# A trunk of two blocks on one core: the second block's adaptive sums on the vector engine behind the norm, one root for two norms, its attention regrouped, weights in 2 MB transfers

## The chip, the cores and the metric

One core of a Trainium2 chip runs the whole program. The metric is the device time of one execution in microseconds (us). Three executions of the kernel before gave a median of 1782.59 us (1780.39 to 1788.25). All arithmetic is float32.

## The reference

A row of 256 tokens of width 1024 passes through two blocks. Every sublayer is `x + gate * f(norm(x) * (1 + scale) + shift)`, where shift, scale and gate are an adaptive product of the conditioning vector with a 1024 x 3072 matrix.

```python
def adaln(cond, w, b):
    mod = cond @ w + b
    shift, scale, gate = jnp.split(mod, 3, axis=-1)
...
def attend(q, k, v):                 # attention a of the second block, 4 heads, two score maps each
    s = jnp.einsum('bqhcd,bkhcd->bhcqk', q, k) * (A_QK ** -0.5)
    p = jax.nn.softmax(s, axis=-1)
    a = p[:, :, 0] - lam * p[:, :, 1]
    return jnp.einsum('bhqk,bkhd->bqhd', a, v)
def post(o):
    o = rmsnorm(o, subln_g) * (1.0 - lam_init)
```

The first block has a Fourier and convolution mixer, a mixture of 16 experts with fixed capacity, a windowed attention and another such mixture. The second block's mixer has four groups of 256 channels: the attention `a` above (keys from 256 context and 256 own tokens), an attention `b` with a windowed bias, a pooling and a long convolution ("hyena"). Then come 16 experts of inner width 512, each token going to two of them, and a last norm.

## The kernel before

The stages run one after the other: mixer 0, experts 0, mixer 1, experts 1, mixer 2, experts of the second block (`moe2`), the last norm. In this profile they are at 0 to 155, 184 to 641, 654 to 772, 799 to 1265, 1266 to 1468 and 1490 to 1765 us.

All weights, 631 MB, come in one fixed order through a ring. `Stream.pump` (L309) issues the next transfer on SP's queue as long as fewer than `RING` slots are taken. A slot is 1 MB, 128 partitions of 2048 floats, and there are 14. `done` frees a slot once its last reader is issued; the transfer that takes its place waits for that reader. The host lays the weights out so that one slot is one contiguous block (`by_rows`, L257).

The adaptive products are cut into steps by `ada_steps` (L480). Where `ON_V` names a part, VectorE adds up the rows of the matrix into the first slot (`add_rows`, L485: the first row of 1024 columns by L492, each further one by L490), and one short set of matmuls with ones sums over the partitions (L497). Elsewhere TensorE does it, for shift and scale at L512 and for the gate at L555. For the second block, keys (2, 0) and (2, 1), TensorE does all of it. `fill` takes the next of these steps wherever the program calls it, so these calls set where the products stand among the other work; `weave` steps through several generators in turn. The order on each engine is then fixed by a scheduler when the program is built.

Mixer 2 (`mixer2`, L1351) takes the roots of two norms, one after the other (`rstd`, `inv_root`), scales, turns and modulates the rows (L648, L659, L671), projects them (L1395 with rope, L1337 for features, L1325 for tokens), and then weaves attention `a` with further projections and hyena with attention `b` and pooling. In both attentions a step is one head of 128 queries: scores (L1436 or L1500), softmax on VectorE and ScalarE, four transposes of the weights (L1419), and four matmuls with the values into 128 queries by 64 channels (L1423). The results of both are then turned at L1373. The output product is L697, the sums over the norm's squares L614.

In `moe2` the router (L681 to L963), a chain of small VectorE operations (L1672 to L1826) and the gathers (L1743) come ahead of the first expert. An expert has L1772 (two products into halves of the columns), L1787 and L1797, and L1802 multiplies by the gate row `hkb`.

```python
RING = 14
ON_V = {(0, 0): "", (0, 1): "s", (1, 0): "g", (1, 1): "sg", (2, 0): "", (2, 1): ""}
```

## Time and profile before

| | |
|---|---|
| median of three executions | 1782.59 us (1780.39 to 1788.25) |
| the profiled execution | 1785.29 us, its span 1783.1 us |
| TensorE (PE) busy | 1421.8 us, 80% of the span |
| VectorE (DVE) / ScalarE (ACT) busy | 455.2 us, 26% / 242.9 us, 14% |
| weights on SP's queue | 630.67 MB, engines taken 86.6% of the span |
| mean granted TensorE clock | 0.857 of full speed |

The profile counts two records for one float32 matmul or weight load of the program (a transpose has one), so "x32" of L697's shape is 16 matmuls. A busy share is an average over stages with different limits, so every stage is read by itself.

### The profile page before, as it was taken

What the parts mean: (1) busy time and instruction counts of PE and PEld (TensorE: products, weight loads), DVE (VectorE), ACT (ScalarE), POOL (GpSimd) and SP (SyncE); (2) the same over time, 40 slices, a digit from 0 to 9 for tenths busy, and PEclk for the clock granted to TensorE, in tenths of its full rate; (3) what the DMA queues carried; (4) which work ended last, traced back from release to release, by engine and by line L of the source; (5) the groups of instructions that cost most, each with busy time, mean ns of one, the idle gap of its engine ahead of it and who ended that gap; (6) DMA issues with size and microseconds to landing.
All of it is one profiled execution on the core that took longest, in us unless ns stands there. A gap on an engine that the chain in (4) does not pass through costs nothing. (4 is left out here: it accounts for less than half of the span.)

```text
span 1783.1 us, 24944 instructions
## 1 busy us (share of the span) xinstructions
PE 1421.8 (80%) x10776; PEld 720.3 (40%) x10776; DVE 455.2 (26%) x1042; ACT 242.9 (14%) x556; POOL 10.7 (1%) x19
## 2 busy tenths in 40 slices
PE   6997877867666679987676776678799998999996
PEld 2444423323222234543232232235477745655453
DVE  2523212401010038541110100100333424333223
ACT  3021100100000012420200000000222312101012
POOL 0000000000000000000000000000000000000000
PEclk9997868878676689998787767868898998999998
DMA  9978899999999999289999999999931566999970
GB/s 375 421 310 325 346 420 421 420 421 421 420 422 421 420 410 408 101 354 420 421 420 421 421 420 421 421 421 420 409 107 51 206 242 239 421 421 415 392 297 25
DMA packets 89746, 635.93 MB, mean 357 GB/s; under 512 B 10944, under 2 KB 11072, under 8 KB 13344
## 3 DMA queue, kind: packets, MB, share of 16 engines
q1 hardware_dynamic: 87392, 630.67, 86.6%
q0 software_dynamic: 1952, 3.09, 0.5%
q8 instruction: 87, 1.43, 0.3%
q10 hardware_dynamic: 288, 0.52, 0.1%
q14 instruction: 27, 0.22, 0.0%
HBM read 633.25 MB, written 1.05 MB: 356 GB/s over the span
## 5 line engine op out<-in xcount | busy, mean ns | idle before, releaser
L1052 PE MATMUL b<-w,xg 128*32 128x256 f32 x4096 | 359.3, 493 | 172.6 <-DMA w<-in_moe_w_up_dram 99.8
L1052 PEld LDWEIGHTS b<-w,xg 128*32 128x32 f32 x4096 | 135.9, 132 | 392.7 <-DMA w<-in_moe_w_up_dram 150.2
L1052 PE MATMUL b<-w,hidT 128*32 128x256 f32 x2048 | 173.8, 476 | 71.5 <-DMA w<-in_moe_w_down_dram 55.3
L1072 DVE TENSOR_TENSOR hid<-b,sg 128x256 f32<-128x256 f32 x32 | 13.6, 425 | 499.0 <-PE b L1052 406.6
L1052 PEld LDWEIGHTS b<-w,hidT 128*32 128x32 f32 x2048 | 64.8, 130 | 166.6 <-DMA w<-in_moe_w_down_dram 95.3
L1772 PE MATMUL u<-w,xg 128*64 128x256 f32 x1088 | 128.0, 383 | 0.0
L1080 DVE SCALAR_TENSOR_TENSOR Y<-b,cc,gq 32x256 f32<-32x256 f32 x128 | 61.5, 481 | 224.2 <-PE b L1052 222.6
L1772 PEld LDWEIGHTS u<-w,xg 128*64 128x64 f32 x1088 | 78.2, 137 | 46.1 <-issue 10.3
L1797 PE MATMUL b<-w,hidT 128*64 128x512 f32 x272 | 65.8, 598 | 6.0 <-ACT hidT L1789 6.0
L1067 ACT ACTIVATE sg<-b 128x256 f32<-128x256 f32 x32 | 12.3, 383 | 424.7 <-PE b L1052 424.7
L697 PE MATMUL b<-w,n 128*128 128x512 f32 x128 | 56.0, 594 | 0.0
L1077 ACT COPY hidT<-b 128x256 f32<-128x256 f32 x32 | 11.9, 372 | 312.2 <-PE b L1075 312.2
L490 DVE SCALAR_TENSOR_TENSOR w<-w,cond 128x1024 f32<-128x1024 f32 x42 | 52.4, 1276 | 1.3 <-DMA w<-in_ada01s_dram 1.2
L1743 PE MATMUL b<-oh,n 128*128 128x128 f32 (+1 forms) x288 | 40.8, 301 | 3.5 <-DVE oh L1737 2.1
L1093 PE MATMUL b<-Y,gT 128*128 128x512 f32 x64 | 35.7, 702 | 9.5 <-DVE Y L1080 9.5
L1174 PE MATMUL b<-w,hT 128*128 128x512 f32 x96 | 43.1, 605 | 0.0
L1743 PEld LDWEIGHTS b<-oh,n 128*128 128x128 f32 x288 | 38.0, 212 | 11.3 <-issue 7.9
L822 PE MATMUL b<-w,hT 128*128 128x512 f32 x96 | 41.6, 593 | 1.1 <-DVE hT L671 1.1
L989 PE MATMUL b<-oh,n 128*128 128x128 f32 x256 | 39.9, 323 | 0.9 <-DVE oh L1032 0.9
L989 PEld LDWEIGHTS b<-oh,n 128*128 128x128 f32 x256 | 37.3, 233 | 7.2 <-issue 5.7
L1325 PE MATMUL b<-pe,w 128*128 128x256 f32 x160 | 38.6, 396 | 0.0
L1802 DVE TENSOR_TENSOR Y<-b,hkb 64x512 f32<-64x512 f32 x34 | 23.4, 688 | 53.6 <-PE b L1797 53.3
(439 smaller groups left out, 1383.9 us busy)
## 6 DMA issues: line engine op xcount, KB each, us to landing
w<-in_moe_w_gate_dram SPq DMA_DIRECT2D x128, 1024.0 KB, 19.8
w<-in_moe_w_up_dram SPq DMA_DIRECT2D x128, 1024.0 KB, 19.8
w<-in_moe_w_down_dram SPq DMA_DIRECT2D x128, 1024.0 KB, 19.8
w<-in_moe_w_dram SPq DMA_DIRECT2D x102, 1024.0 KB, 10.4
w<-in_wi_dram SPq DMA_DIRECT2D x10, 1024.0 KB, 19.8
w<-in_ada00s_dram SPq DMA_DIRECT2D x8, 1024.0 KB, 18.5
w<-in_ada01s_dram SPq DMA_DIRECT2D x8, 1024.0 KB, 20.6
w<-in_ada10s_dram SPq DMA_DIRECT2D x8, 1024.0 KB, 7.0
```

Source lines behind the costliest of these rows:

```text
L490: V.scalar_tensor_tensor(into[:, hs], w[:, hs], c, into[:, hs], op0=OP.mult, op1=OP.add)
L697: T.matmul(acc, mixT[:, kt, b * 128:(b + 1) * 128], w(kt)[:, h * 512:(h + 1) * 512], start=kt == first, stop=kt == last)
L822: T.matmul(p, hT[:, kt, b * 128:(b + 1) * 128], w(kt), start=kt == 0, stop=kt == 7)
L989: T.matmul(p[:, j * 128:(j + 1) * 128], n[:, b, dt * 128:(dt + 1) * 128], oh[:, b, g * 128:(g + 1) * 128], start=b == 0, stop=b == 1)
L1052: T.matmul(p[32 * q:32 * q + 32, :256], lhs(kt), w[:, k, q * 256:(q + 1) * 256], start=kt == 0, stop=kt == 7)
L1080: V.scalar_tensor_tensor(Y[32 * j:32 * j + 32, q * 256:(q + 1) * 256], pd[32 * q:32 * q + 32, :256], cc[32 * q:32 * q + 32, e:e + 1], gq[3 ...
L1093: T.matmul(p, gT[:, b * 128:(b + 1) * 128], Y[:, h * 512:(h + 1) * 512], start=True, stop=True)
L1174: T.matmul(p, hT[:, kt, b * 128:(b + 1) * 128], w(kt), start=kt == 0, stop=kt == 7)
L1325: T.matmul(p[:, j * 256:(j + 1) * 256], w(kt)[:, c0 + j * 128:c0 + (j + 1) * 128], h[:, kt], start=kt == 0, stop=kt == 7)
L1743: T.matmul(p[:, j * 128:j * 128 + m], n[:, b, dt * 128:(dt + 1) * 128], oh[:, b, :m], start=b == 0, stop=b == 1)
L1772: T.matmul(p[rows[h], :256], xg[:, kt, c], w[kt // 4][:, kt % 4, h * 256:(h + 1) * 256], start=kt == 0, stop=kt == 7)
L1797: T.matmul(pd[rows[h]], hidT[:, kt % 2, rows[kt // 2]], w[kt // 2][:, kt % 2, h * 512:(h + 1) * 512], start=kt == 0, stop=kt == 3)
```

## The change

1. A transfer carries two slots, 2 MB with 16 KB for each partition, and the ring has 7 such tiles. A tile is freed when both halves are. What came alone (`tpc`, `dft`, `l0c`, `wbias`, `pool`) takes a whole tile; the two filter packs become one.
2. The second block's adaptive sums except shift and scale of (2, 0) go to VectorE: 8 + 16 + 8 operations on 1024 columns, and 4 + 4 + 2 matmuls with ones. `queue_behind` makes them stand behind the last VectorE operation of mixer 2's modulation, and in `moe2` behind the first gather's last `ohg`.
3. Both norms' mean squares stand in one tile of four columns, with one root.
4. A step of attention `a` is two heads, four score banks. The values are the stationary operand: two heads' products go to the two column halves, 64 channels by 128 queries, so the results come out turned; the norm of `a` and the division of `b` are applied through `spread`, 8 matmuls of 64 x 128 that copy a factor per head and query over the channels.
5. The calls of `fill` move: none before mixer 2's projections, five steps beside attention `a`, the rest beside hyena and `b`; in `moe2` the gate's steps come after the first pair's gather.

```diff
-ON_V = {(0, 0): "", (0, 1): "s", (1, 0): "g", (1, 1): "sg", (2, 0): "", (2, 1): ""}
-RING = 14
+ON_V = {(0, 0): "", (0, 1): "s", (1, 0): "g", (1, 1): "sg", (2, 0): "g", (2, 1): "sg"}
+RING = 7
...
     def pump(self):
-        while self.issued < len(self.order) and self.issued - len(self.freed) < RING:
...
+        while self.issued < len(self.order):
+            if self.issued - sum(all(k in self.freed for k in keys) for keys, _, _ in self.order[:self.issued]) >= RING:
+                return
+            keys, shapes, ap = self.order[self.issued]
+            t = self.pool.tile([128, 2 * SLOT], F32, name="w")
+            self.nc.sync.dma_start(t[:, :ap.shape[1]], ap)
...
         def add_rows(kt, w, into):
+            with ExitStack() as behind:
+                if queue_behind:
+                    behind.enter_context(tc.issue_after(queue_behind[-1].ins))
+                add_rows_(kt, w, into)
...
-            r1 = rstd(ss)
...
-            r2 = inv_root(r2)
-            V.tensor_tensor(r2, r2, r1, op=OP.mult)
-            fill(4)
+            ms = small.tile([128, 4], F32, name="r2")
...
+            rs = inv_root(ms, 4)
+            r1, r2 = rs[:, 0:2], rs[:, 2:4]
             scale_rows(n, x, r2)
-            modulate(hT, turn(n), ada[2, 0])
+            queue_behind.append(modulate(hT, turn(n), ada[2, 0]))
             scale_rows(x, x, r1)
-            fill_until(lambda: ((2, 0), "g", 3) in st.freed)
...
-                    T.matmul(po[:, h * 64:(h + 1) * 64], eT[:, kb * 128:(kb + 1) * 128], vals[:, kb, h * 64:(h + 1) * 64],
-                             start=kb == 0, stop=kb == 3)
+                    for u in range(2):
+                        h = 2 * j + u
+                        T.matmul(po[64 * u:64 * u + 64, at:at + 128], vals[:, kb, h * 64:(h + 1) * 64],
+                                 ets[u][:, kb * 128:(kb + 1) * 128], start=kb == 0, stop=kb == 3)
...
+                    pp = [bank() for _ in range(4)]
+                    for i in range(4):
+                        T.matmul(pp[i], qT[32 * i:32 * i + 32, j, qb * 128:(qb + 1) * 128], kT[32 * i:32 * i + 32, j], start=True, stop=True)
...
             def after_a():
+                A.activation(sq, oa, AF.Square)
...
-                t4(mixT[:, 0:2], lambda b: oa[:, b])
...
+                  fills(5))
+            fill_until(lambda: (2, 0) in gqs and ((2, 0), "g", 0) in st.freed)
+            weave(hyena(), attention_b(), after_a(), chain(pooling(), filling(1, (2, 1))))
...
-            fill(1)
             nT = [wk.tile([128, 8, 128], F32, name="xg", bufs=2) for _ in range(2)]
...
-            fill(99)
...
             ts = {0: pair(0)}
+            queue_behind.append(ts[0]["last"])
+            fill(99)
```

The change moves instructions. In its program the lines stand 10 to 35 further down: L555's work is L506 and L499, L659 is L668, L1395 L1404, L1436 L1463, L1419 L1428, L1423 L1440, L697 L707.

TensorE at the start of mixer 2, before (from the experts' last combination to the first scores):

```order
L1093 MATMUL b<-Y,gT 128x512 x4
L555 MATMUL b<-w,cond_both 32x256 x24
L659 MATMUL b<-cst,n 128x128 x6
L555 MATMUL b<-w,cond_both 32x256 x8
L659 MATMUL b<-cst,n 128x128 x10
L1395 MATMUL b<-w,pe 128x256 x32
L1337 MATMUL b<-w,pe 128x256 x16
L1325 MATMUL b<-pe,w 128x256 x16
L1373 MATMUL b<-cst,pe 128x128 x8
L1436 MATMUL b<-kT,qT 128x512 x4
L1325 MATMUL b<-pe,w 128x256 x8
L1419 MATMUL b<-cst,pe 128x128 x4
```

And in the changed kernel:

```order
L1103 MATMUL b<-Y,gT 128x512 x4
L668 MATMUL b<-cst,n 128x128 x16
L1404 MATMUL b<-w,pe 128x256 x32
L1347 MATMUL b<-w,pe 128x256 x16
L1335 MATMUL b<-pe,w 128x256 x16
L1383 MATMUL b<-cst,pe 128x128 x8
L1463 MATMUL b<-kT,qT 128x512 x8
L1335 MATMUL b<-pe,w 128x256 x16
L1428 MATMUL b<-cst,pe 128x128 x8
```

The 32 matmuls of the gate of (2, 0) are gone from around the transposes, and two steps of scores, eight banks, now stand in front of the next projection.

TensorE beside attention `b` and hyena, before (L512 is the shift and scale of (2, 1)):

```order
L1500 MATMUL b<-bk,bq 128x256 x4
L512 MATMUL b<-w,cond 32x512 x4
L1613 MATMUL b<-pe,w 128x256 x2
L1419 MATMUL b<-cst,pe 128x128 x3
L1613 MATMUL b<-pe,w 128x256 x6
L1419 MATMUL b<-cst,pe 128x128 x5
L512 MATMUL b<-w,cond 32x512
L1423 MATMUL b<-bv,pe 128x64 x8
L512 MATMUL b<-w,cond 32x512 x3
L1590 MATMUL b<-kT,w 128x256 x8
```

In the changed kernel, from attention `b`'s first scores (L1504 sums the squares of `a` over half the partitions, L1449 is `spread`):

```order
L1528 MATMUL b<-bk,bq 128x256 x8
L1504 MATMUL b<-cst,pe 128x2 x4
L1576 MATMUL b<-w,hcT 64x256 x8
L1610 MATMUL b<-kT,w 128x256 x8
L1428 MATMUL b<-cst,pe 128x128 x8
L1440 MATMUL b<-pe,bv 64x128
L1449 MATMUL b<-cst,root 64x128 x3
L1440 MATMUL b<-pe,bv 64x128 x7
L1449 MATMUL b<-cst,root 64x128 x5
```

No adaptive matmul is left between hyena's products and the attention, and L1504, which waits for ScalarE's square, stands in line ahead of hyena's L1610.

VectorE at the first gather of `moe2` in the changed kernel (L501 and L499 are the adaptive sum's operations, L1775 the modulated gather, L1762 and L1779 the one-hot tiles of the next pairs, L1809 an expert's hidden product); before, none of the sums stood there:

```order
L501 TENSOR_SCALAR w<-w,cond 128x1024
L1775 TENSOR_SCALAR xg<-b,shsc_7141 128x128
L499 SCALAR_TENSOR_TENSOR w<-w,cond 128x1024
L1775 TENSOR_SCALAR xg<-b,shsc_7141 128x128 x2
L499 SCALAR_TENSOR_TENSOR w<-w,cond 128x1024
L1775 TENSOR_SCALAR xg<-b,shsc_7141 128x128
L499 SCALAR_TENSOR_TENSOR w<-w,cond 128x1024
L1762 TENSOR_SCALAR oh<-cst,rank 128x64
L499 SCALAR_TENSOR_TENSOR w<-w,cond 128x1024
```

The sums now stand between the four evacuations that the first expert's products read.

## Rows read from the trace of the kernel before

**Rows 1.** The page: GB/s in 40 slices of 44.6 us each.

```profile
GB/s 375 421 310 325 346 420 421 420 421 421 420 422 421 420 410 408 101 354 420 421 420 421 421 420 421 421 421 420 409 107 51 206 242 239 421 421 415 392 297 25
```

**Rows 2.** DMA view of 250 to 600 us: all transfers, then SP's queue (packets, MB, share).

```profile
DMA packets 20207, 147.31 MB, mean 421 GB/s; under 512 B 2244, under 2 KB 2244, under 8 KB 2244
q1 hardware_dynamic: 20187, 147.00, 101.0%
```

**Rows 3.** Windows: stretch, its length, busy time per engine, clock, DMA share, GB/s.

```profile
1263.00:1286.00 23.00, 15.48 (x106) 7.16 (x107) 12.73 (x33) 8.97 (x22) 0.00 (x0) 0.68 1.01 420
1286.00:1382.00 96.00, 92.27 (x426) 72.14 (x425) 29.36 (x70) 23.32 (x55) 0.00 (x0) 0.95 0.27 97
1382.00:1440.00 58.00, 57.16 (x340) 38.78 (x339) 23.98 (x54) 18.52 (x40) 1.59 (x3) 1.00 0.69 245
1345.00:1356.00 11.00, 8.83 (x26) 6.02 (x26) 3.80 (x9) 1.93 (x5) 0.00 (x0) 0.54 0.16 63
1468.00:1498.00 30.00, 21.85 (x146) 15.34 (x144) 17.71 (x93) 6.49 (x15) 0.00 (x0) 0.83 0.54 205
1498.00:1740.00 242.00, 233.57 (x1604) 130.86 (x1602) 66.92 (x152) 30.32 (x73) 0.00 (x0) 1.00 0.94 382
```

**Rows 4.** Timeline of PE at mixer 2's start: start, length, line, idle before it.

```profile
1263.35 1.94 PE L1052 MATMUL b<-w,hidT 128*32 128x256 f32 x16 [0.55 <-DMA w<-in_moe_w_down_dram]
...
1281.42 1.51 PE L659 MATMUL b<-cst,n 128*128 128x128 f32 x6 [4.57 <-DVE n L648]
1282.87 1.83 PE L555 MATMUL b<-w,cond_both 128*32 128x256 f32 x16
```

**Rows 5.** Timeline of DVE in the two chained roots.

```profile
1277.83 0.16 DVE L1379 TENSOR_TENSOR r<-ss 128x2 f32<-128x2 f32 x1 [0.51 <-ACT b L614]
...
1280.53 0.75 DVE L648 TENSOR_SCALAR n<-x,root 128x1024 f32<-128x1024 f32 x1
```

**Rows 6.** Timeline of PE in attention `a`.

```profile
1315.22 1.14 PE L1436 MATMUL b<-kT,qT 32*128 32x512 f32 x8 [0.78 <-ACT kT L1374]
...
1346.51 1.11 PE L1419 MATMUL b<-cst,pe 128*128 128x128 f32 x4 [1.44 <-DVE pe L1452]
1348.36 1.97 PE L1423 MATMUL b<-va,pe 128*128 128x64 f32 x8 [0.73 <-ACT pe L1421]
...
1352.26 5.62 PE L1325 MATMUL b<-pe,w 128*128 128x256 f32 x16
...
1361.39 3.72 PE L1325 MATMUL b<-pe,w 128*128 128x256 f32 x16
```

**Rows 7.** PE groups by shape, 1300 to 1440 us: busy time, mean ns, idle before.

```profile
L1436 PE MATMUL b<-kT,qT 32*128 32x512 f32 x32 | 13.3, 702 | 0.8 <-ACT kT L1374 0.8
L512 PE MATMUL b<-w,cond 128*32 128x512 f32 x64 | 12.5, 603 | 0.0
...
L1423 PE MATMUL b<-va,pe 128*128 128x64 f32 x64 | 9.7, 299 | 0.7 <-ACT pe L1421 0.7
L1423 PE MATMUL b<-bv,pe 128*128 128x64 f32 x64 | 8.3, 278 | 0.7 <-ACT pe L1421 0.7
```

**Rows 8.** Timeline of PE in `moe2`: 32 matmuls into halves of the columns.

```profile
1647.10 7.08 PE L1772 MATMUL u<-w,xg 128*64 128x256 f32 x64
```

**Rows 9.** The page's group of VectorE's adaptive sums.

```profile
L490 DVE SCALAR_TENSOR_TENSOR w<-w,cond 128x1024 f32<-128x1024 f32 x42 | 52.4, 1276 | 1.3 <-DMA w<-in_ada01s_dram 1.2
```

**Rows 10.** DMA view of 697 to 800 us: issues, KB each, median us to landing.

```profile
w<-in_ada20s_dram SPq DMA_DIRECT2D x8, 1024.0 KB, 7.9
```

**Rows 11.** Timeline of DVE: the first two maxima of attention `a`.

```profile
1316.38 1.29 DVE L1442 TENSOR_REDUCE nm<-b 128x1 f32<-128x512 f32 x2 [14.57 <-PE b L1436]
```

**Rows 12.** Timeline of DVE in `moe2`'s router chain.

```profile
1483.11 0.69 DVE L563 TENSOR_TENSOR hkb<-b,hkb 128x512 f32<-128x512 f32 x1 [2.02 <-PE b L555]
```

**Rows 13.** Groups by shape, 1500 to 1760 us: PE's waits in the experts.

```profile
L1797 PE MATMUL b<-w,hidT 128*64 128x512 f32 x256 | 62.1, 598 | 5.5 <-ACT hidT L1789 5.5
...
L1787 PE MATMUL b<-cst,hid 128*128 128x128 f32 x32 | 7.0, 299 | 2.9 <-DVE hid L1783 2.9
```

More of the change, by code (lines that the diff above doesn't have):

```diff
@@ L80, in main_consts @@
     p.add("tri", (i[:, None] < i[None]).astype(float))
+    p.add("half", (i[:, None] // 64 == np.arange(2)[None]).astype(float))
     p.add("invf", np.tile(inv.astype(np.float32)[None], (128, 1)))
@@ L309, in pump @@
     def pump(self):
[L310 to L318 removed]
+        while self.issued < len(self.order):
[4 more added lines that the diff above has]
+            self.nc.sync.dma_start(t[:, :ap.shape[1]], ap)
+            for i, (key, shape) in enumerate(zip(keys, shapes)):
+                v = t[:, i * SLOT:i * SLOT + int(np.prod(shape))]
+                self.tiles[key] = v.rearrange("p (a b) -> p a b", a=shape[0]) if len(shape) == 2 else v
             self.issued += 1
@@ new lines, in mixer2, with scores, softmax @@
+            steps = [(qb, j) for qb in range(2) for j in range(2)]
+            def attention_a():
+                es = {}
+                po = bank()
+                def scores(qb, j):
+                    pp = [bank() for _ in range(4)]
+                    for i in range(4):
+                        T.matmul(pp[i], qT[32 * i:32 * i + 32, j, qb * 128:(qb + 1) * 128], kT[32 * i:32 * i + 32, j], start=True, stop=True)
+                    return pp
+                def softmax(pp, qb, j):
+                    nm = small.tile([128, 4], F32, name="nm2")
+                    for i in range(4):
+                        V.tensor_reduce(nm[:, i:i + 1], pp[i], axis=AX.X, op=OP.max, negate=True)
@@ new lines, in softmax @@
+                    e = []
+                    for i in range(4):
+                        e.append(temp())
+                        A.activation(e[i], pp[i], AF.Exp, scale=32 ** -0.5, bias=nm[:, i:i + 1], accum_out=den[:, i:i + 1])
+                    d = den.rearrange("p (u c) -> p c u", c=2)
+                    V.tensor_copy(den0[:, qb, 2 * j:2 * j + 2], d[:, 0])
+                    cf = small.tile([128, 2], F32, name="cf")
+                    V.reciprocal(cf, d[:, 1])
+                    V.scalar_tensor_tensor(cf, cf, lam, d[:, 0], op0=OP.mult, op1=OP.mult)
@@ L1466, in attention_a @@
+                    for u in range(2):
+                        V.scalar_tensor_tensor(e[2 * u], e[2 * u + 1], cf[:, u:u + 1], e[2 * u], op0=OP.mult, op1=OP.add)
+                    es[qb, j] = e[0::2]
                 softmax(scores(*steps[0]), *steps[0])
-                for t in range(8):
-                    if t < 7:
+                for t in range(4):
+                    if t < 3:
                         pp = scores(*steps[t + 1])
                     yield
-                    values(*steps[t])
-                    if t < 7:
+                    attend(po, es.pop(steps[t]), va, *steps[t])
+                    if t < 3:
@@ L1530, in attention_b @@
                     yield
-                    values(*steps[t])
+                    attend(po, es.pop(steps[t]), bv, *steps[t])
                     if t < 3:
@@ L1536, in attention_b @@
                         st.done(("wb", 0))
-                t4(mixT[:, 2:4], lambda b: ob[:, b])
-                after_a()
+                f = temp()
+                A.copy(f, spread(rd))
+                V.tensor_tensor(mixT[:, 2:4].rearrange("p j s -> p (j s)"), po, f, op=OP.mult)
             def short(g, j0):
@@ L1865, in pair @@
                 t = tiles()
-                take([(rank[:, :, e], gates[:, :, e]) for e in (e0, e0 + 1)], t)
+                t["last"] = take([(rank[:, :, e], gates[:, :, e]) for e in (e0, e0 + 1)], t)
                 return t
```

214 lines of the change are left out of this document (93 added, 121 removed).

## The prediction

> **What bounds the kernel now.** I read the page's slices first. Two long plateaus at 420 to 422 GB/s are the experts of the first block [rows 1]; the DMA view of one of them shows SP's queue taking 101.0% of the engines [rows 2], so there the weights are the bound and nothing an engine saves is worth anything. From the page's slices those plateaus are about 205 to 640 and 825 to 1263 us, 873 us together. The windows say what the second block is [rows 3]. From 1286 to 1440 us TensorE is busy 92.27 of 96 and 57.16 of 58 us while DMA stands at 97 and 245 GB/s: the ring is full and TensorE is the bound. At 1263 to 1286 (norm and roots) and 1468 to 1498 us (router) nothing is busy throughout and chains of small operations set the time, at a granted clock of 0.68 and 0.83. From 1498 to 1740 us TensorE is busy 233.57 of 242 us at 382 GB/s: TensorE first, transfers close behind. So the change can gain in the second block by taking work off TensorE, and what decides is whether waits appear where that work stood.
>
> **The transfers.** Bytes and their order stay. No row moves 16 KB for a partition, so the new rate is bounded by its neighbours. Below stand the page's slices of 410 GB/s at the ends of the plateaus [rows 1]: 873 x (421/410 - 1), +23 us. Above, of 20,207 packets 2,244 are under 512 bytes and close the transfers [rows 2]; half of them go, and if each took as long as one of data, 5.6% of 873 us would, -49. By their bytes, 512 at most, it is 0.4%. I take that, -3.5, since the engines' time follows the bytes at a steady 421. The Trainium skill ("DMA: Bandwidth & Descriptors", the fit under "Anatomy of one DMA") gives each transfer a fixed 2.0 us beside bytes / 436 GB/s; by it two slots in one transfer would cost 6.8 instead of 8.8 us, a quarter less. The rows have 1 MB in 2.49 us already (1.05 MB at 421 GB/s), so that fixed part is hidden, and the sum goes without it.
>
> A tile counts as landed only when both halves are. At the end of a plateau TensorE then has two slots to work through after the last landing instead of one: the last eight matmuls took 1.94 us [rows 4], 1 to 2 us more in each of two stages. At the start of each, the first freed tile needs both halves read, about 1 us. Together +5. In mixer 0 the last tile of the first shift and scale likewise leaves four more matmuls behind its landing, +1.
>
> **Mixer 2's start.** One root replaces two chained ones: from the second sum to the scaled rows took 2.70 us [rows 5], of which one square root and about three VectorE steps go, -0.65. The gate's last eight matmuls stood among the transposes for 1.83 us [rows 4]; they go. But the others kept TensorE at work before the wait of 4.57 us [rows 4]; without them it idles from 1272 us on, and the transposes begin at the low clock. I take -1.0 in all, between -2.5 and +1.
>
> **Projections and attention `a`.** Scores: four matmuls of 32 rows side by side took 1.14 us [rows 6], 1.07 from start to start, while all 16 took 13.3 us [rows 7], since later ones stood singly. Four groups of four are 4.3 us: -9.0. The Trainium skill ("TensorE: Matmul & The Clock Gate", part 3) measured four such matmuls 3.07 times as fast as singly; from the 1.05 us of a lone one the 16 would be 5.5 us by that. The row of this kernel decides. Values: 64 columns are half of the array; 32 matmuls of 256 columns into alternating halves took 7.08 us [rows 8], 0.22 each, so eight of 128 columns are about 0.9 us. Four steps are 3.6 against 9.7 us [rows 7]: -6.1. The two waits of 1.44 and 0.73 us and the clock of 0.54 that follows them [rows 3, 6] belong to the old grouping; sixteen records of L1325 took 5.62 instead of 3.72 us there: -4.6 for the whole dip. Added are four matmuls with ones, +0.5.
>
> Here a new wait comes in. The order puts two steps of scores, all eight banks of the kernel's pool, before the next projection, which therefore waits for the first exponential. Maxima take 0.64 us each and the first starts 1.16 us after the scores [rows 6, 11]. Four of them, the scaling and one exponential (taken as long as a maximum) end some 4.8 us after the scores start, and TensorE has 2.1 us of scores: +2.7. A wait of 1.44 us was followed by a clock of 0.54 for about 10 us [rows 3, 6], so I add +4.0 for a dip of that kind. This part: -9.0 - 6.1 - 4.6 + 0.5 + 2.7 + 4.0 = -12.5.
>
> VectorE has the room: its 24 sums of 1.28 us [rows 9] are 31 us beside 53 busy of 154 [rows 3]. Before rope six sums delay VectorE by at most 7.7 us, while TensorE has 21 us of projections, so they cost nothing. If ada21s lands late, VectorE waits in front of a softmax: a transfer of half the size took 7.9 us when alone [rows 10]. In attention `a` the next softmax has about that in hand.
>
> **Attention `b`, hyena, pooling.** L512 is busy for 12.5 us [rows 7], some 11.7 without the overlap of neighbouring records; it goes. Values go from 8.3 [rows 7] to 3.6, eight turnings go (1.2, from six transposes in 1.51 us at the low clock, [rows 4]); `spread` adds two times 0.9, the ones matmuls and the half sums 1.4. TensorE's work: -14.4. But L512 was also what TensorE did while softmax and hyena's VectorE steps ran. Now L1504 stands in line behind ScalarE's square, and the square behind the two exponentials of `b`'s first step: scores of 1.1 us, two maxima and their biases, two exponentials and the square, at 0.4 to 0.7 us each, end some 5 us after the scores start, of which TensorE has 2 covered, +3.0. VectorE's sums of the third ada21s tile come before those maxima and wait for a transfer issued late, +1.6. Hyena's products wait for VectorE operations that now stand behind `b`'s reciprocals and biases, and the last step and the ones matmuls wait for their softmax and copy: five waits of 0.4 to 1.3 us, +4.0. A clock dip as above, +4.0. This part: -1.8; without the dip and half of the waits it would be -10.
>
> **Router and `moe2`.** VectorE's chain stood 2.02 us for the gate and 0.69 in adding it [rows 12]; that moves behind the gather, -2.7. The table for roots, loaded earlier before, is now loaded right after the sums of squares, +0.9, and without the gate's matmuls TensorE's transposes and router products run at the low clock longer, +1.3. Sum -0.5. In `moe2` the first expert's inputs stand between sums of 1.28 us on VectorE and two ones matmuls wait for all eight sums, +2.9. The order of the later pairs has `hid` and `hidT` waited for in the open from the second pair on, where TensorE had 8.4 us of such waits [rows 13]: about 5 more waits of 0.55, less what fewer changes between shapes give back, +1.1. Sum +4.0. At the start five tiles of expert weights are in the ring instead of 14 slots; with TensorE asking for 382 of 421 GB/s [rows 2, 3] this lead is enough.
>
> **The sum.** +1.0 + 5.0 - 3.5 - 1.0 - 12.5 - 1.8 - 0.5 + 4.0 = -9.3 us against the profiled execution of 1785.3, which makes 1776.0. That execution is 2.7 above the median of the runs shown; against the median of 1782.6 the forecast is **1773.3 us**. A measurement of this kernel can tell about 0.5%, 9 us, from no change.
>
> **The rivals.**
> - *The work comes off whole.* No clock dips follow the new waits (-8) and the waits are half as long (-4): 1761 us. For it: the wait of 0.78 us at 1314 [rows 6] left the clock alone. Against it: the dip after 1.44 us.
> - *Attention `b` and hyena become chains.* TensorE waits in many pieces and falls to the low clock again and again in what was 1382 to 1440 us: a clock of 0.54 as at 1345 [rows 3] on 16 us of its work costs 16/0.54 - 16, 13.6 instead of the 4.0 taken, which makes 1783, no change. For it: with L512 gone softmax and hyena's steps have no cover, and that stretch was 98% busy [rows 3]. Against it: most of the work still stands between the waits. The Trainium skill ("TensorE: Matmul & The Clock Gate", part 1) says that the array falls to half its clock when it idles; by that rule this is what taking filler out costs, and [rows 3] agree with their 0.54.
> - *The larger transfers are slower.* 16 KB a partition at 410 GB/s: +23 in place of -3.5, 1800 us, slower than before. It decides from about 414 GB/s downwards, 873 x (421/414 - 1) = 15 us in place of -3.5. For it only the slices at the ends of the plateaus [rows 1]; against it the steady 420 to 422 between.
> - *`moe2` starves.* The gate's two tiles hold 4.2 MB of the ring into the first expert; if transfers then end last, the stage ends 4.2 MB / 421 GB/s later, +10: 1783. Against it: 382 GB/s asked [rows 3].
>
> **Chances.** Forecast 0.45, work comes off whole 0.25, chains 0.14, `moe2` starves 0.06, slower transfers 0.10. The forecast's own range is 1765 to 1781, and rather more than half of it lies below 1773.7, which is faster by 0.5%: 0.25, with the whole gain's 0.25 and 0.02 of the others 0.52. Slower by 0.5% (above 1791.5) are most of the slower transfers and the far end of the chains, 0.12. The rest, 0.36, is the same. The range that leaves out 2 in 10 reaches from 1755 to 1790.
>
> **What would show it.** After the change the two plateaus should show the rate (0.4% more taken); at 1310 to 1320 us TensorE should wait for the first exponential before the projection and the clock row dip after it; the scores should stand in groups of 1.1 us and the values at 0.9; L1504 should wait for ScalarE; in the router no wait for `hkb`. The forecast is wrong if the plateaus change by more than 5 us each, if mixer 2 from 1266 to 1440 us is not 12 to 20 us shorter, or if `moe2` is longer by more than 8.

## The result, and the profile after

The changed kernel takes **1761.98 us** (median of 4 runs, 1761.46 to 1762.87) against 1781.71 for the kernel before (4 runs): ratio 0.9883, 95% interval 0.9858 to 0.9907, 21 us faster by the ratio. The forecast was 1773.3 with a range of 1755 to 1790. The profiled execution took 1761.91 us with a span of 1760.0, so the sum is compared span with span: -23.1 us measured, -9.3 forecast.

The page of the changed kernel, GB/s in 40 slices of 44 us, and all packets:

```profile
GB/s 375 407 276 396 326 427 427 428 427 427 427 427 428 427 415 336 145 305 426 426 426 427 427 428 427 427 427 427 418 78 144 267 229 188 427 427 427 423 306 26
DMA packets 46973, 636.03 MB, mean 361 GB/s; under 512 B 6192, under 2 KB 6320, under 8 KB 8464
```

The plateaus stand at 427 where they stood at 421 [rows 1]. The DMA view of 250 to 600 us of the changed kernel, as [rows 2]:

```profile
DMA packets 10272, 149.57 MB, mean 427 GB/s; under 512 B 1142, under 2 KB 1142, under 8 KB 1142
q1 hardware_dynamic: 10252, 149.26, 100.3%
```

Half the packets for 1.5% more bytes. The windows of the second block, with the columns of [rows 3]: mixer 2's start, projections and attention `a`, attention `b` with hyena, the output projection and router, the experts.

```profile
1259.00:1276.00 17.00, 7.35 (x25) 4.84 (x26) 10.96 (x26) 9.23 (x22) 0.00 (x0) 0.70 0.96 406
1276.00:1359.00 83.00, 78.06 (x409) 63.16 (x408) 43.73 (x76) 21.83 (x51) 0.00 (x0) 0.98 0.27 95
1359.00:1413.50 54.50, 49.32 (x342) 38.32 (x341) 32.18 (x60) 22.30 (x45) 1.59 (x3) 0.97 0.73 289
1413.50:1471.00 57.50, 43.53 (x175) 27.33 (x174) 21.51 (x91) 9.97 (x21) 0.00 (x0) 0.82 0.36 139
1471.00:1710.00 239.00, 226.71 (x1580) 129.34 (x1580) 76.07 (x166) 28.44 (x71) 0.00 (x0) 1.00 0.97 405
```

In the second and third stretch TensorE does about 22 us less work than in 92.27 + 57.16 us before, but it now idles 5 us in each. The timeline of PE at the waits that the forecast named (start, length, line, in brackets the idle time before):

```profile
1272.48 3.47 PE L668 MATMUL b<-cst,n 128*128 128x128 f32 x16 [9.31 <-DVE n L657]
...
1305.23 2.00 PE L1463 MATMUL b<-kT,qT 32*128 32x512 f32 x16 [0.78 <-ACT kT L1384]
1309.94 8.76 PE L1335 MATMUL b<-pe,w 128*128 128x256 f32 x32 [2.71 <-ACT pe L1475]
...
1373.59 1.05 PE L1504 MATMUL b<-cst,pe 128*128 128x2 f32 x8 [2.65 <-ACT pe L1500]
1374.57 3.66 PE L1576 MATMUL b<-w,hcT 128*64 128x256 f32 x16
...
1389.40 1.10 PE L1633 MATMUL b<-pe,w 128*128 128x256 f32 x4 [1.51 <-DVE pe L1617]
```

2.71 us before the projection and 2.65 before the half sums: both new waits are there, at the forecast length (2.7 and 3.0). What follows each is slower: L1335's 32 records 8.76 instead of 7.17 us, L1576's 16 records 3.66 instead of the 2.00 of the same product before. That is 1.6 and 1.7 us, not the 4.0 each that I had put down for a clock dip. The groups of PE by shape, 1290 to 1415 us, as [rows 7], and those of the last stage, 1473 to 1735 us, as [rows 13]:

```profile
L1440 PE MATMUL b<-pe,va 128*64 128x128 f32 x64 | 6.1, 282 | 0.4 <-ACT pe L1430 0.3
L1440 PE MATMUL b<-pe,bv 128*64 128x128 f32 x64 | 5.7, 281 | 0.2 <-ACT pe L1430 0.2
L1463 PE MATMUL b<-kT,qT 32*128 32x512 f32 x32 | 4.3, 626 | 0.8 <-ACT kT L1384 0.8
...
L1823 PE MATMUL b<-w,hidT 128*64 128x512 f32 x256 | 59.5, 598 | 9.3 <-ACT hidT L1815 9.3
L1813 PE MATMUL b<-cst,hid 128*128 128x128 f32 x32 | 6.7, 290 | 4.1 <-DVE hid L1809 4.1
```

Scores are at the forecast 4.3 us. Values take 6.1 and 5.7, not 3.6.

The stages of the runs, in us, from the start times of TensorE's first matmul of each (first expert of block one; end of block one's last expert; first projection of mixer 2; first scores of `a`; first of `b`; output projection; first expert of the last stage; end). Left out is only the step from projection to scores, 29.4 to 30.7 everywhere.

| kernel | mixer 0 | block one's experts, mixer 1 | mixer 2 start | `a` | `b` | output, router | last stage |
|---|---|---|---|---|---|---|---|
| before | 183.7 | 1081.6 | 20.5 | 73.9 | 51.1 | 57.6 | 285.4 |
| before_again | 181.1 | 1083.0 | 20.4 | 74.2 | 51.1 | 57.9 | 285.4 |
| slots_2mb_alone | 181.7 | 1075.8 | 17.6 | 75.9 | 51.1 | 57.9 | 280.2 |
| **changed** | 182.8 | 1075.3 | 17.6 | 63.7 | 44.5 | 57.9 | 288.7 |
| after_again | 183.0 | 1076.3 | 17.7 | 64.2 | 46.4 | 58.6 | 287.8 |
| slots_1mb | 179.6 | 1083.1 | 17.8 | 63.8 | 44.5 | 58.7 | 290.2 |
| old_attention | 182.0 | 1076.2 | 17.8 | 76.3 | 47.4 | 57.4 | 290.5 |
| sums_tensor | 182.7 | 1075.7 | 16.2 | 61.9 | 53.4 | 58.4 | 280.2 |
| first_gate_back | 181.7 | 1076.0 | 16.2 | 58.2 | 46.4 | 58.7 | 280.2 |

### The profile page after: what moved, and what is told of

Read it like the earlier page. It is cut to its first block, busy times and chain, and to the rows that moved or that the text cites. A ratio compares the mean times of both kernels' runs of the same rounds, so it can differ in the third digit from the quotient of the medians.

```text
span 1760.0 us, 24127 instructions
## 1 busy us (share of the span) xinstructions
PE 1321.3 (75%) x10668; PEld 724.1 (41%) x10668; DVE 485.0 (28%) x1055; ACT 245.9 (14%) x559; POOL 10.7 (1%) x19
## 5 line engine op out<-in xcount | busy, mean ns | idle before, releaser
L1062 PE MATMUL b<-w,xg 128*32 128x256 f32 x4096 | 326.8, 476 | 218.3 <-DMA w<-in_moe_w_up_dram 128.7
L1062 PEld LDWEIGHTS b<-w,xg 128*32 128x32 f32 x4096 | 151.6, 131 | 390.7 <-issue 150.6
L1062 PE MATMUL b<-w,hidT 128*32 128x256 f32 x2048 | 158.5, 462 | 79.3 <-DMA w<-in_moe_w_down_dram 70.7
L1062 PEld LDWEIGHTS b<-w,hidT 128*32 128x32 f32 x2048 | 74.5, 128 | 150.8 <-DMA w<-in_moe_w_down_dram 60.9
L499 DVE SCALAR_TENSOR_TENSOR w<-w,cond 128x1024 f32<-128x1024 f32 x70 | 88.0, 1279 | 6.2 <-DMA w<-in_ada21s_dram 4.7
L707 PE MATMUL b<-w,n 128*128 128x512 f32 x128 | 56.0, 594 | 0.0
L1768 PEld LDWEIGHTS b<-oh,n 128*128 128x128 f32 x288 | 36.9, 209 | 9.5 <-issue 6.7
L1335 PE MATMUL b<-pe,w 128*128 128x256 f32 x160 | 38.5, 396 | 2.7 <-ACT pe L1475 2.7
L1103 PE MATMUL b<-Y,gT 128*128 128x512 f32 x64 | 30.6, 611 | 9.6 <-DVE Y L1090 9.6
L1823 PEld LDWEIGHTS b<-w,hidT 128*64 128x64 f32 x272 | 18.7, 136 | 42.1 <-issue 28.2
L707 PEld LDWEIGHTS b<-w,n 128*128 128x128 f32 x128 | 24.0, 190 | 28.8 <-issue 28.7
```

What stands on the lines that cost most here:

```text
L499: V.scalar_tensor_tensor(into[:, hs], w[:, hs], c, into[:, hs], op0=OP.mult, op1=OP.add)
L707: T.matmul(acc, mixT[:, kt, b * 128:(b + 1) * 128], w(kt)[:, h * 512:(h + 1) * 512], start=kt == first, stop=kt == last)
L1062: T.matmul(p[32 * q:32 * q + 32, :256], lhs(kt), w[:, k, q * 256:(q + 1) * 256], start=kt == 0, stop=kt == 7)
L1103: T.matmul(p, gT[:, b * 128:(b + 1) * 128], Y[:, h * 512:(h + 1) * 512], start=True, stop=True)
L1335: T.matmul(p[:, j * 256:(j + 1) * 256], w(kt)[:, c0 + j * 128:c0 + (j + 1) * 128], h[:, kt], start=kt == 0, stop=kt == 7)
L1768: T.matmul(p[:, j * 128:j * 128 + m], n[:, b, dt * 128:(dt + 1) * 128], oh[:, b, :m], start=b == 0, stop=b == 1)
```

## The experiments

Each ratio is to the kernel before on the same chip, with its 95% interval.

**slots_1mb**, the changed kernel with its transfers undone (below, in part), and **slots_2mb_alone**, the kernel before with nothing but them (the same lines the other way round):

```diff
-RING = 7
+RING = 14
-            t = self.pool.tile([128, 2 * SLOT], F32, name="w")
-            self.nc.sync.dma_start(t[:, :ap.shape[1]], ap)
+            t = self.pool.tile([128, SLOT], F32, name="w")
+            self.nc.sync.dma_start(v, flat)
```

> The changed kernel with the transfers as before: 1 MB each, 14 slots in the ring; attention, sums and root stay changed. Theory (the larger transfers run at 427 instead of 421 GB/s and that is all they do): both plateaus go back to 421 GB/s, the first block's experts become about 4 and 2 us longer, the rest within 1, in all 1768 us against 1762 of the changed kernel. Rival A (the tail and the start of the larger tiles give the rate back, as the forecast had it with +5.0 against -3.5): no difference or 1 to 2 us shorter, 1761. Rival B (the ring's seven large tiles are also what makes the last stage longer): the last stage from the first expert's matmul to the end, 288.7 us in the changed kernel, gets 2 to 4 us shorter again.

> The kernel before with only the transfers changed: 2 MB each, seven tiles in the ring. Theory: plateaus at 427 GB/s, 5 to 7 us off the first block, nothing else, 1782 - 6 = 1776 us. Rival A (rate given back at the tails): 1781 to 1783. Rival C (the second block's last stage starves with seven tiles when the old order of its sums stands): its stage of 285.3 us gets 5 us or more longer and the total comes to 1781 although the plateaus are shorter.

slots_1mb: 1770.13 us, 0.9922 [0.9904, 0.9940]. slots_2mb_alone: 1770.55 us, 0.9930 [0.9911, 0.9950]. Their slices of GB/s, in this order:

```profile
GB/s 372 421 309 341 369 420 421 421 421 421 421 421 421 420 409 408 120 312 420 421 420 421 421 420 421 421 421 421 406 241 214 103 156 204 421 422 420 416 305 25
```

```profile
GB/s 379 399 288 379 348 426 427 428 426 427 427 427 429 426 410 340 96 368 427 427 426 427 428 425 428 428 427 427 378 71 48 197 296 232 428 427 409 391 346 26
```

421 with 1 MB, 427 with 2 MB, whatever else stands in the program. Block one's stretch is 1081.6 to 1083.1 us in the three profiles with 1 MB and 1074.8 to 1077.1 in the eleven with 2 MB: the transfers give about 7 us there, and the rival that tails give it back is out. So are the two rivals on the last stage: with seven large tiles it is not longer (288.7 against 290.2 us, and 280.2 against 285.4). But alone the transfers are worth 12 us, not 6: mixer 2's start is 2.9 shorter and the last stage 5.2. At the start, the fixed order of the kernel before had the matmuls of the last of four 1 MB gate tiles among the transposes [rows 4], although that tile had landed at 1278.2 us, 3.2 before the transposes began; with two larger tiles the order has all of them ahead. Of the 5.2 us, 3.2 are a clock dip in the last expert that the profile of slots_2mb_alone does not have (more on it at the end), so they cannot be put down to the transfers. In the changed kernel that gate is not on TensorE, and the last stage is long for another reason (below), so there the same transfers are worth only 5 to 8 us: the parts of the change overlap.

**old_attention**, the recast undone (`attend`, `scores`, `softmax`, `after_a` and the end of `attention_b` as in the kernel before):

```diff
-            weave(attention_a(), (chain(...), 2), fills(5))
+            weave(attention_a(), (chain(...), 1), fills(5))
-            weave(hyena(), attention_b(), after_a(), chain(pooling(), filling(1, (2, 1))))
+            weave(hyena(), attention_b(), chain(pooling(), filling(1, (2, 1))))
```

> The changed kernel with the attentions as before (scores of two heads at a time, values with 64 columns per head, normalisation before the transposes); transfers, sums on VectorE and the single root stay. Theory (the recast carries attention a): from the first projection of mixer 2 to that of the context tiles some 9 to 11 us come back (scores 13 us busy again instead of 4.3, values 9.7 instead of 6), attention b and hyena 2 to 4 us more, in all 1762 + 12 to 15 = 1774 to 1777. Rival (the sums taken off TensorE carry the gain of mixer 2 and the recast only trades scores for waits): at most +5, 1767.

1778.05 us, 0.9973 [0.9963, 0.9983]: 14 to 16 us come back by the ratios, 12 to 13 of them in `a` and 1 to 3 in `b`. Its groups by shape, 1306 to 1430 us:

```profile
L1444 PE MATMUL b<-kT,qT 32*128 32x512 f32 x32 | 13.3, 702 | 0.8 <-ACT kT L1383 0.8
L1431 PE MATMUL b<-va,pe 128*128 128x64 f32 x64 | 9.7, 299 | 0.7 <-ACT pe L1429 0.7
L1431 PE MATMUL b<-bv,pe 128*128 128x64 f32 x64 | 8.3, 277 | 1.5 <-ACT pe L1429 1.4
```

13.3 - 4.3 = 9.0 us are scores and 9.7 - 6.1 = 3.6 values. The old grouping's clock dip is still there (0.66 in 1336 to 1347 us), and the recast removes it, at the price of its own waits. The recast carries attention `a`.

**sums_tensor**, the second block's sums back on TensorE, at their old places:

```diff
-ON_V = {..., (2, 0): "g", (2, 1): "sg"}
+ON_V = {..., (2, 0): "", (2, 1): ""}
```

> The changed kernel with the second block's adaptive sums on TensorE, at the places they had before; transfers, recast attention and single root stay. Theory (the sums were cover as well as work): attention b and hyena get 11.7 us of matmuls back, of which the waits now open there (some 5) are covered again, +6 to +8; the router gets its 2.7 us wait back, the last stage loses its 3.4, mixer 2's start is 1 to 2 us longer: in all +6 to +9, 1768 to 1771. Rival A (the cover was worth all of it): 0 to +2, 1763. Rival B (all 23 us of those matmuls lie on the path): +18 or more, 1780.

1759.63 us, 0.9866 [0.9845, 0.9886]: none of the three. It is no slower than the changed kernel (the intervals overlap; the medians differ by 2 to 4 us). The table says why: moving the sums to VectorE gains 7 to 9 us in `b`, and costs 1.4 at mixer 2's start, 2 in `a` and 8 in the last stage. The window of `b` in sums_tensor, then in the changed kernel:

```profile
1366.00:1419.00 53.00, 49.40 (x335) 32.31 (x336) 19.98 (x46) 18.89 (x39) 1.59 (x3) 0.94 0.56 214
```

```profile
1369.00:1413.00 44.00, 38.89 (x279) 29.58 (x279) 25.56 (x51) 18.65 (x39) 1.59 (x3) 0.96 0.68 264
```

TensorE has 10.5 us less to do and the stretch is 9 shorter: in `b` the sums had been almost no cover at all.

**after_again** and **before_again**, unedited, for the spread:

> The changed kernel once more, unedited, to see how far two profiled executions of one program differ by stage. Theory (the first mixer's stage differs between executions by chance: 179.6 to 183.7 us in five profiles whose code there does the same work): this stage comes out anywhere between 179 and 184, every later stage within 0.5 us of the changed kernel's first profile (experts 454.0 and 464.7, attention a 63.7, attention b 44.5, last stage 288.7), total 1759 to 1763. Rival (each of these differences is made by the code): the first stage repeats at 182.8 within 0.5.

> The kernel before once more, unedited, for the spread of its stages. Theory (the first mixer's stage differs by chance between executions, every later one repeats): first stage 179 to 185 us, experts 457.8 and 466.4 within 0.8, mixer 2's start 20.5, attention a 73.9, attention b 51.1, last stage 285.4, each within 0.8. Rival (the start of mixer 2 at 20.5 was chance too, and is 17 to 18 as in the kernel with only the transfers changed).

after_again: 1763.26 us, 0.9893 [0.9877, 0.9909]. before_again: 1784.34 us, 1.0006 [0.9993, 1.0018]. The changed kernel's mixer 0 repeated at 183.0, which the rival had too and which decides nothing; the kernel before's did not repeat (183.7 and 181.1), and the clock of its last stretch differs with it. The windows of before and of before_again:

```profile
155.00:184.00 29.00, 19.12 (x122) 16.97 (x126) 12.76 (x48) 6.27 (x14) 0.00 (x0) 0.59 0.50 209
```

```profile
155.00:184.00 29.00, 18.00 (x182) 14.20 (x178) 15.23 (x55) 9.03 (x18) 0.00 (x0) 0.76 0.60 242
```

That is not the whole cause: profiles with 0.76 in this window have mixer 0 anywhere from 179.6 to 183.0 us. So nothing under 3 us is read from mixer 0. Mixer 2's start of 20.4 is not chance. Against the expectation, after_again's `b` was 1.9 us longer (clock 0.93 against 0.96), its router 0.7 longer and its last stage 0.9 shorter, where 0.5 was allowed; so 2 us is what one profile tells in `b`, and 1 us elsewhere.

**no_bank_wait**, both new waits taken away by order alone:

```diff
                 softmax(scores(*steps[0]), *steps[0])
+                yield
                 for t in range(4):
...
                 A.activation(sq, oa, AF.Square)
+                yield
...
-            weave(hyena(), attention_b(), after_a(), chain(pooling(), filling(1, (2, 1))))
+            weave(after_a(), hyena(), attention_b(), chain(pooling(), filling(1, (2, 1))))
```

> The changed kernel, where attention a gives up its turn once between its first softmax and its second group of scores, so that a projection stands between the two groups, and where the half sums' square is issued ahead of attention b's exponentials, with its matmuls one turn later. Theory (both new waits, 2.7 us before the projection and 2.65 us before the half sums, are idle time on the path): attention a from its first scores to attention b's first scores 63.7 - 2.7 to 4.4 = 59.3 to 61.0 us, attention b to the output projection 44.5 - 2.7 to 4.3 = 40.2 to 41.8, total 1753 to 1757. Rival A (the waits only move: the later softmax, whose VectorE queue holds the sums, is late by as much): both stages within 1 us, total 1761 to 1762. Rival B (order changes what later stages wait for): a gain in a or b that is lost again behind it.

1760.06 us, 0.9881 [0.9866, 0.9897], against 0.9883 and 0.9893. PE's timeline:

```profile
1302.74 1.14 PE L1463 MATMUL b<-kT,qT 32*128 32x512 f32 x8 [0.78 <-ACT kT L1384]
1303.81 7.17 PE L1335 MATMUL b<-pe,w 128*128 128x256 f32 x32
1310.91 1.14 PE L1463 MATMUL b<-kT,qT 32*128 32x512 f32 x8
...
1367.41 1.05 PE L1506 MATMUL b<-cst,pe 128*128 128x2 f32 x8
1368.32 3.70 PE L1612 MATMUL b<-kT,w 128*128 128x256 f32 x16
...
1382.49 2.04 PE L1635 MATMUL b<-pe,w 128*128 128x256 f32 x4 [3.65 <-DVE pe L1619]
...
1441.87 3.68 PE L691 MATMUL b<-cst,n 128*128 128x128 f32 x16 [5.42 <-DVE n L657]
1445.34 3.44 PE L952 MATMUL b<-vec,shsc 128*128 128x16 f32 x16
1448.70 1.94 PE L967 MATMUL b<-xg,sg 128*32 128x128 f32 x32
```

Both waits are gone. In `a` the theory holds: 60.8 us, 2.9 to 3.4 less. In `b` rival A does: 45.3, between the two profiles of the changed kernel. The wait for hyena's products, 1.51 us there, is 3.65 here. VectorE's timeline shows what they wait for, in the changed kernel:

```profile
1380.19 0.69 DVE L1615 TENSOR_TENSOR pe<-b,hkc 128x512 f32<-128x512 f32 x1
1386.22 0.17 DVE L1543 RECIPROCAL rdb<-den 128x2 f32<-128x2 f32 x1 [5.34 <-ACT pe L1541]
```

and in no_bank_wait:

```profile
1376.36 0.17 DVE L1545 RECIPROCAL rdb<-den 128x2 f32<-128x2 f32 x1 [2.50 <-ACT pe L1543]
1378.87 0.43 DVE L1540 TENSOR_TENSOR b<-b,w 128x256 f32<-128x256 f32 x1 [2.34 <-PE b L1530]
1379.21 0.68 DVE L1617 TENSOR_TENSOR pe<-b,hkc 128x512 f32<-128x512 f32 x1
```

In both, hyena's steps stand in VectorE's order behind operations of `b` that wait for an exponential or for scores, while their own inputs (L1610's and L1612's products, done at 1381.9 and 1372.0 us) are ready: L1616 starts at 1387.4 and L1617 at 1379.2. So a wait ahead of that was worth nothing in `b`. Whether another order on VectorE would shorten `b` was not tried.

Nor does the gain in `a` reach the total. The output and router stage is 60.2 us, where the two profiles of the changed kernel have 57.9 and 58.6. Behind the same wait (5.42 and 5.41 us) the router's L952 and L967 take 3.44 and 1.94 us, against 1.86 and 1.08 in the changed kernel. That is rival B's outcome for most of the 3 us; why TensorE is slow for longer there is not shown.

**gate_in_mixer**, the last gate's sums finished inside mixer 2:

```diff
                     out_part(acc[b, h], mixT, "wo", b, h, range(4, 8), 4, 1)
+            fill(99)
...
             queue_behind.append(ts[0]["last"])
-            fill(99)
```

> The changed kernel with the last gate's sums finished inside mixer 2: the remaining steps are issued between the two halves of the output projection, where VectorE is idle, instead of after the first pair's gather. Theory (in the last stage the 8.5 us by which it is longer than with the sums on TensorE, 288.7 against 280.2, come from the sums standing behind the gather: two slots of the ring stay held, the first transfers of expert weights are issued 20 us later, and the matmuls of the later pairs stand in an order with open waits): the last stage falls to 280 to 283 us, the output projection and router stay within 1.5 us, total 1753 to 1756. Rival A (only the four matmuls with ones and their wait move): the last stage 286 to 288, total 1760. Rival B (the vector engine has no room beside the projection and the residual adds): the stage from the output projection to the first expert, 57.9 us, grows by 4 or more.

1759.31 us (1754.02 to 1764.68), 0.9870 [0.9847, 0.9893]. The last stage is 280.4 us as the theory has it, output and router 58.9; in total less shows than the 8 us, since the executions of this kernel spread most (its profile has mixer 0 at clock 0.59, 184.8 us). The groups of [rows 13] in this kernel:

```profile
L1824 PE MATMUL b<-w,hidT 128*64 128x512 f32 x270 | 63.5, 597 | 8.0 <-ACT hidT L1816 8.0
L1814 PE MATMUL b<-cst,hid 128*128 128x128 f32 x34 | 7.2, 294 | 3.5 <-DVE hid L1810 3.5
```

3 us of the 8 are waits for `hid` and `hidT` (over the whole stage 15.2 us of gaps against 18.1) and 1.2 the four matmuls with ones behind the first expert's. About 3 are a clock dip: TensorE's last 64 `u` matmuls took 9.11 us in the changed kernel and 7.13 here, behind the same wait of 2.06 us, with 1.1 more in the gather ahead of them. So the place of the sums accounts for the waits and the matmuls, some 4 to 5 us. The dip goes with it in the profiles with 2 MB transfers, but slots_1mb has the sums behind the gather too and no dip, so its cause is open. That the ring's hold causes the order with more waits was the theory's reason and is not shown by this run.

**scale_sums_only**, both gates on TensorE at their old places, the second shift and scale on VectorE:

```diff
-ON_V = {..., (2, 0): "g", (2, 1): "sg"}
+ON_V = {..., (2, 0): "", (2, 1): "s"}
```

> The changed kernel with only the second shift and scale summed on VectorE (the 1024-column pairs that attention b's stretch had as matmuls); both gates are on TensorE at the places they had before. Theory (each of the three sets of sums has its own balance: the shift and scale's come off the path in attention b, 8.9 us; the first gate's cost 1.4 at the start of mixer 2 and 1.8 in attention a; the second gate's cost 8.5 in the last stage): mixer 2's start 16.2, attention a 61.9, attention b 44.5, last stage 280.2, total 1757.9 - 8.9, about 1751 as timed. Rival A (the sums' gain in attention b needs the first gate's early place on VectorE too): attention b 48 or more. Rival B (the ring moves differently and the last stage stays at 288): 1757 to 1759.

1758.01 us, 0.9863 [0.9847, 0.9879], where 1751 was expected. Mixer 2's start is 16.2 and `b` 46.1, but `a` is 68.3 us instead of 61.9. VectorE's timeline there:

```profile
1311.68 0.75 DVE L501 TENSOR_SCALAR w<-w,cond 128x1024 f32<-128x1024 f32 x1 [2.04 <-DMA w<-in_ada21s_dram]
...
1336.49 3.68 DVE L499 SCALAR_TENSOR_TENSOR w<-w,cond 128x1024 f32<-128x1024 f32 x3 [5.22 <-DMA w<-in_ada21s_dram]
...
1349.58 3.68 DVE L499 SCALAR_TENSOR_TENSOR w<-w,cond 128x1024 f32<-128x1024 f32 x3 [1.61 <-DMA w<-in_ada21s_dram]
```

ScalarE's and TensorE's behind it:

```profile
1355.27 0.56 ACT L1567 ACTIVATE hcT<-b,vec 128x256 f32<-128x256 f32 x1 [8.17 <-DVE hcT L1569]
```

```profile
1356.36 0.66 PE L1430 MATMUL b<-cst,pe 128*128 128x128 f32 x4 [4.68 <-ACT pe L1432]
```

The sums came early, and VectorE stood 8.9 us for their weights. The first two of these waits left TensorE at work. Behind the third, a step of hyena on VectorE (L1569) was queued behind four sums; ScalarE stood 8.17 us for it, with the copy of attention `a`'s turned weights (L1432) behind, and TensorE 4.68 us for that copy. So this is the hazard of the forecast's "if ada21s lands late", but it came through hyena and ScalarE's queue and not through a softmax, and at a place where the changed kernel avoids it. Neither rival's stage came out: `b` stayed under 48 and the last stage under 288. The last stage's 285.1 has the clock dip again (last 64 matmuls 8.66 us).

**both_moved** takes the two edits that shortened a stage; **first_gate_back** has the first gate on TensorE besides, and holds the shift and scale's sums until `a`'s third softmax; **first_gate_back_2** is the same program on another chip.

```diff
-ON_V = {..., (2, 0): "g", (2, 1): "sg"}
+ON_V = {..., (2, 0): "", (2, 1): "sg"}
...
                     es[qb, j] = e[0::2]
+                    if (qb, j) == steps[2]:
+                        queue_behind.append(v)
```

> The changed kernel with the two edits that shortened a stage: attention a gives up its turn between its first softmax and its second group of scores, and the last gate's sums finish inside mixer 2. Theory (the two gains lie on one path after another and add): attention a 60.8 us, attention b 44.5, last stage 280.3, total 1762 - 2.9 - 8.4 = 1751, between 1749 and 1754. Rival (what is taken out of one stage is waited for in a later one, as the half sums' wait was): 1756 or more.

> The same two edits, and the first gate's sums back on TensorE ahead of the norm; the second shift and scale's sums queue behind attention a's third softmax, so that VectorE cannot stand waiting for their weights ahead of a softmax. Theory (the first gate's sums cost 1.4 us at mixer 2's start and 1.8 in attention a when they stand on VectorE, and the 6.4 that the shift and scale's sums cost in attention a when they came early was VectorE waiting for their transfers): mixer 2's start 16.2, attention a 59 to 60, attention b 44 to 46, last stage 280.3, total 1747 to 1750. Rival (sixteen sums in the shorter time delay hyena's products): attention b 48 or more, total 1751 to 1755.

> The fastest version once more on another chip: 0.981 of the kernel before, within 0.002; attention a 58.2, attention b 46.4, last stage 280.2, each within 0.5. Rival (part of its gain was that one chip's or execution's): 0.984 or more.

both_moved: 1752.64 us, 0.9831 [0.9812, 0.9850]; `a` 60.6, `b` 44.8, last stage 280.2: the gains add, but output and router are 61.2 us, 2.6 to 3.3 longer than in the changed kernel, with L952 and L967 slow as in no_bank_wait. first_gate_back: 1748.87 us, 0.9809 [0.9790, 0.9828]; a second time 1751.90, 0.9835 [0.9812, 0.9858], the same stages to 0.3 us but a ratio between expectation and rival. `a` is 58.2 us, 5.5 shorter than in the changed kernel, and output and router are back at 58.7. The two edits that it has beyond both_moved were not run apart. Its windows: mixer 2's start, projections and `a`, `b`:

```profile
1258.00:1274.00 16.00, 9.62 (x89) 5.23 (x90) 11.17 (x27) 8.46 (x20) 0.00 (x0) 1.00 1.00 424
1274.00:1362.00 88.00, 86.56 (x466) 70.54 (x466) 41.36 (x77) 25.84 (x60) 0.00 (x0) 1.00 0.37 136
1362.00:1408.00 46.00, 40.68 (x281) 30.91 (x278) 33.52 (x59) 18.73 (x39) 1.59 (x3) 0.93 0.66 251
```

The clock is 1.00 where it was 0.70 and 0.98, and TensorE idles 1.4 us in 88. This is the fastest version, about 12 us ahead of the changed kernel by the mean of two ratios of each.

## Why the forecast held in range and direction, and failed in its sizes

The measured time lies in the range, 11 us under the forecast. None of the forecast's own signs of being wrong came: mixer 2 up to the output projection is 19.6 us shorter (12 to 20 said), the two stages of block one's experts changed by 3.8 and 1.7 us, the last stage by 3.3. But most of its terms were off, and some of the total is luck. Point by point, span against span:

- **The transfers** (forecast +5.0 - 3.5, measured -6.3 here, -6.7 by the means of three and eleven profiles). This is the step that failed. I took the closing packets at their bytes, 0.4%, and let everything else follow the bytes at 421; the rate rose by 427/421, 1.4%, which over 873 us is 12. The packets of SP's queue in the trace, 250 to 600 us, show where it comes from: the closing packets (4 bytes) took 9 to 10 ns each, so they were priced well enough, but a data packet of 16,384 bytes took 615.6 ns, where two of 8,192 took 627.9. By these times nearly all of the gain is in the larger data packets, which the forecast had at nothing. The Trainium skill ("DMA: Bandwidth & Descriptors", "The descriptor swizzle") counts for a transfer of 1 MiB to 128 partitions 8 pairs of data and one completion descriptor per engine; the traces agree, 2244 small to 17,943 packets of data with 1 MB and, with 2 MB, 1142 to 9110. Of the 12 us some 7 stayed: about 4 in the first stage of experts and less than 1 in the second, at whose start 298.5 instead of 300.7 MB had moved (5 us at the new rate), and about 2 in mixer 1. So the +5.0 was about right, but nearly all of it is the start of the second stage; why the ring had less ahead there was not tested.
- **Mixer 2's start** (forecast -1.0, measured -2.9, outside its range of -2.5 to +1). The gate leaving the transposes was priced; that the larger transfers alone would do the same (17.6 us with the gate on TensorE) was not seen. From the second sum to the scaled rows the root took 1.84 instead of 2.70 us. With the larger transfers, the gate's place on VectorE costs 1.4: the 16 transposes take 3.47 us behind 9.31 us of idling and 2.05 in sums_tensor. That TensorE idles there and is slow afterwards was the forecast's argument. The Trainium skill ("TensorE: Matmul & The Clock Gate", part 1) says that an idle array falls to half its clock; this row agrees, with a granted clock of 0.70 in the window from 1259 us and of 0.55 over the transposes.
- **Projections and attention `a`** (forecast -12.5, measured -12.7): a sum of errors that cancel. Scores (-9.0) and the bank wait (2.7) were right to a tenth. Values are -3.6, not -6.1: a step's 16 records take 1.09 us in one piece, not 0.9, and here they stand between matmuls of a projection in two pieces of 0.43 and 1.09. The dip cost 1.6, not 4.0. VectorE's sums, "cost nothing", cost 2 us here, their matmuls with ones included: sums_tensor has 61.9. And 2.5 us of the -12.7 only moved: in the changed kernel the last step of `a` (1.04 us of turns, 1.52 of values) runs behind the projection that ends this stretch. With it counted here, this stretch is about -10 and the next about -6.6.
- **Attention `b`** (forecast -1.8, measured -4.0 for the stretch of the forecast, from 1381.7 and 1359.0 us to the output projection). L1504 behind the square was there with 2.65 us (3.0 taken), but taking its wait away gained nothing in `b`. The third ada21s tile, at +1.6, held nothing up: its sums ended as the first scores did. Of the small waits (+4.0) the long one is 1.51 us before hyena's products, and the dip was 1.7, not 4.0.
- **Router** (forecast -0.5): +0.3. Its terms came, the wait for `hkb` with -2.6, the table with +0.9, the low clock in the transposes and router products with +1.5; 0.5 more is a slower gather. **Last stage** (forecast +4.0): +3.3 by its size, but made of -5 (the larger transfers, 3.2 of it a clock dip that is gone) and +8.5 (the gate's sums behind the gather, 3.3 of it the same dip). Without the dip they are about -2 and +5. The right number had two wrong halves.

The rival "the work comes off whole", 1761, is where the time came out, and only in part for its reason: the dips behind the new waits were 1.6 and 1.7 us instead of 4.0 each, but the two longest waits came at their forecast length, and of the 13.8 us by which the spans' differences part (23.1 and 9.3) 7.8 are the transfers in block one. The other rivals are out: no slower transfers, no chain at low clock (0.97 in `b`'s window), no starving (405 GB/s in the last stage's window, and no wait of its matmuls for DMA). Several parts were bundled in this change. The one its name puts first, the sums on VectorE, brought nothing as a whole; the single root had no run of its own.

## What to carry to other kernels

Work moved off the bounding engine pays only where that engine has no slack and the receiving queue has some: here the same kind of sum gained 8 us in one stage and lost as much in another (3 of them in a clock dip), which only a table by stage shows. Moving a sum is cheap where its weights have landed and nothing urgent is queued behind it; a late transfer holds whatever stands behind the sum, here a step of hyena and through it ScalarE and TensorE. Before taking a wait away, ask what stands behind it: of two waits of 2.7 us one was worth 3 in its stage and the other nothing, and in that run most of the 3 was lost again two stages later.

## What the hardware did that I had not expected

- 16 KB rows in 2 MB transfers ran at 427 GB/s, 8 KB rows in 1 MB at 421, both with the queue at its full share (100.3% and 101.0%); one packet of 16 KB took 12 ns less than two of 8 KB. The Trainium skill ("DMA: Bandwidth & Descriptors", "Where 436 GB/s comes from") puts the ceiling of this path at 435 GB/s and says that about 358 binds a transfer from HBM; the rows, one core running, stand close to the first and above the second.
- The clock's answer to the same wait differs: behind 2.06 us in the last stage, the last 64 `u` matmuls took 7.13 us in seven profiles and 7.9 to 9.4 in the other seven. sums_tensor and scale_sums_only run the same last stage, and its end from that wait on differs by 4.9 us: gather and `u` matmuls take 3.79 and 7.13 us in the one, 6.94 and 8.66 in the other. It is not chance from one execution to the next, as far as three pairs show: from the gather to the end of these matmuls it is 14.30 and 14.31 us in the two profiles of the kernel before, 14.34 and 14.35 in those of the changed one, and 11.06 twice in the fastest version. What in a program decides it is open, so a few us of it can be neither credited nor charged to an edit of that stage.
